# A decoder step on one core: the dense expert stage's loads ordered behind the last projections' loads, and the finishing loads spread over blocks

## The chip, the cores and the metric

The kernel runs on one core of one Trainium2 chip. The core has TensorE (PE in the tables, PEld for its weight loads), VectorE (DVE), ScalarE (ACT), GpSimd (POOL) and SyncE (SP). Here SP computes nothing: it issues nearly all loads and stores, in the order of its program, and an instruction that has to wait holds up everything behind it. GpSimd issues the indirect gathers on a queue of its own. The metric is the device time of one execution in microseconds, as the median of the runs.

## The reference, cut to what matters

One decoder layer is applied to 64 sample tokens and 512 prompt tokens, D = 1024, all in float32. After a mixer (an S5 group and an RWKV-7 group) each token gets a channel mixer that retrieves experts:

```python
x = x + ga1 * (concat([y_s5, y_rw]) @ w_out)
h = rmsnorm(x, norm2_g) * (1 + sc2) + sh2
q = (h @ w_q).reshape(T, 8, 2, 64)                      # 8 heads, two halves of a key
s1, s2 = q[:, :, 0] . keys1, q[:, :, 1] . keys2         # 128 scores each
# top 16 of s1 and of s2, the 256 sums of them, top 16 of these: 16 of 16384 experts per head
act = gelu(u_tab[idx] . h)
ff  = sum over the 8 x 16 chosen experts of gate * act * v_tab[idx]
y   = rmsnorm(x + ga2 * ff, final_norm_g)
```

## The kernel before, in words

The 576 tokens are five tiles: tile 0 holds the 64 sample tokens, tiles 1 to 4 are 128 prompt tokens each. They go through the mixer in the order 1, 2, 3, 0, 4 (`ORDER`), several stages of different tiles woven together by generators.

`select` (L1201) makes a tile's output projection, its norm, the query projection and the scores. It streams its weights through two buffers of 512 KB with the tag "w": eight `wo`, `ga1`, `sh2`, eight `wq` (L1267, used at L1269), and `keys` last (L1273, used at L1285). A load into one of the two buffers waits until PE (or another reader) is done with what was in it. `pick` (L1292) finds the top experts, almost all of it on DVE.

The experts of tiles 1 to 3 (`DENSE`) are not gathered but computed densely. `gbuild` (L1463) writes a table of gates into DRAM (`Gd`), and `dense` (L1538) runs over all 16384 experts in 128 blocks of 128. For block b:
- `ublock` (L1498) loads 512 KB of u (`ur`, two buffers), splits it into a high part on ACT (`uh`, L1504) and a low part on DVE (`ul`, L1505), and PE makes `pd`, 24 matmuls (L1508). `first(b + 1)` calls it one block ahead.
- ACT applies Gelu (`wf`, L1587), DVE multiplies by the gates `Gr` (L1589), and the result is split again (`wh`, `wl`).
- 512 KB of v (`vr`, two buffers, L1599) are loaded and split likewise (`vh`, `vl`), and PE adds 18 matmuls to the sums `po` (L1607).
- `loadG` (L1561) fetches the gates `Gr` of eight blocks at a time, 1536 KB in rows of 512 bytes, into one of two buffers.

Beside the dense blocks go the selection of tile 4 (`pick`, three steps a block) and `bulk` (L1425), which gathers the experts of tiles 0 and 4 row by row: 384 gathers of 512 KB from GpSimd, each consumed by one DVE instruction (L1441 or L1451), three a block. At block 32 (`FB`) `open_finish` (L1389) loads what `finish` (L1404) needs for the last addition and norm of all five tiles: the rows `fx` of each tile, the gates `fg` of prompt and samples, and the norm's weights `gF`.

The program's order on an engine is made when the kernel is built, by a planner that simulates the engines and takes, among what it holds ready, what was traced first. So a load whose buffer is free early may be put ahead of loads that were traced long before it. `tc.issue_after(ins)` adds an order without a wait: what the block traces on the engine of `ins` comes after `ins` in that engine's program.

Of the kernel before, what the change touches and what calls it, by code (L numbers as in the profile page):

```python
# [147 lines left out]
def weave(tc, *parts):  # L148
    live = [[p[0], p[1], 0.0, p[2], p[3] if len(p) > 3 else 0] for p in parts]
    while any(p[3] for p in live):  # L150
        for p in list(live):
            p[2] += p[1]
            while p[2] >= 1:
                p[2] -= 1
                try:
                    if p[4]:
                        with tc.high_priority(offset=p[4]):
                            next(p[0])
                    else:
                        next(p[0])  # L160
                except StopIteration:
                    live.remove(p)
                    break
# [14 lines left out]
class Kernel:  # L178
# [3 lines left out]
    GBL = 8  # L182
# [1018 lines left out]
    def select(self, ti):  # L1201
        yo = self.yo.pop(ti)
        nc, I, O = self.nc, self.I, self.O
        V, S, G, T, SY = nc.vector, nc.scalar, nc.gpsimd, nc.tensor, nc.sync
        t2, t4, ps, ident, sm = self.t2, self.t4, self.ps, self.ident, self.sm
        sw = self.sw
        smp = ti == 0
# [62 lines left out]
                yield  # L1270
            S.copy(qT[:, 4 * q:4 * q + 4, :], pt)
        keys = self.ws.tile([128, 8, 128], F32, name="keys", tag="w", bufs=2)
        SY.dma_start(keys, I["keys"])  # L1273
        sc4 = []
        for g0 in range(0, 4 if smp else 8, 4):
            for sd in range(2):
# [112 lines left out]
    def open_finish(self):  # L1389
        SY = self.nc.sync  # L1390
        self.sf = Scope(self.tc)
        f = self.fin = self.sf.pool("fin", side="right", reuse_waits="tile")
        self.fx = {}
        for ti in list(self.ORDER):
            self.fx[ti] = f.tile([128, D], F32, name="fx%d" % ti)
            SY.dma_start(self.fx[ti], self.x1d[ti])
        self.fg = {}
        for smp in (False, True):
            self.fg[smp] = f.tile([128, D], F32, name="fg%d" % smp)
            self.mod(self.fg[smp], 3, smp)  # L1400
        self.gF = f.tile([128, D], F32, name="gF")
        SY.dma_start(self.gF, self.I["rows"][1:2, :].to_broadcast([128, D]))

    def finish(self, ti, ffs, add=None):  # L1404
        nc, O = self.nc, self.O
        V, S = nc.vector, nc.scalar
        smp = ti == 0
        nr = 64 if smp else 128
        c0 = 0 if smp else 64 + 128 * (ti - 1)
        x1, ga2 = self.fx[ti], self.fg[smp]  # L1410
        tmp = self.fin.tile([128, D], F32, name="ft", bufs=2)
        w = D // len(ffs)
        for n, f in enumerate(ffs):
            V.tensor_tensor(tmp[:nr, n * w:(n + 1) * w], f, ga2[:nr, n * w:(n + 1) * w], op=OP.mult)
        (add or V).tensor_tensor(x1[:nr], x1[:nr], tmp[:nr], op=OP.add)
        ss = self.sm.tile([128, 1], F32, name="ss")
        S.activation(tmp[:nr], x1[:nr], AF.Square, accum_out=ss[:nr])
        self.rstd(ss, ss, 1e-6, nr, self.sm)
        V.scalar_tensor_tensor(x1[:nr], x1[:nr], ss[:nr], self.gF[:nr], op0=OP.mult, op1=OP.mult)
        nc.sync.dma_start(O["y_all"][c0:c0 + nr, :], x1[:nr])  # L1420
# [117 lines left out]
    def dense(self):  # L1538
        nc, I, O = self.nc, self.I, self.O
        V, S, G, T, SY = nc.vector, nc.scalar, nc.gpsimd, nc.tensor, nc.sync  # L1540
        nd, TG, GBL = len(self.DENSE), self.TG, self.GBL
        N = 128 * nd
        S.copy(self.dh, self.hf)
        V.tensor_tensor(self.dl, self.hf, self.dh.bitcast(F32), op=OP.subtract)
        self.sh.close()
        ux = len(self.wu)
        kw = dict(reuse_waits="tile")
        sp = self.sp = Scope(self.tc)
        ue = self.ue if self.EU else sp.pool("ue", **kw)
        up = sp.pool("up", 2, **kw)  # L1550
        dp = self.dp if self.ED else sp.pool("dp", 1, **kw)
        pso = sp.pool("pso", 1, space=PSUM, **kw)
        self.gb = sp.pool("gb", **kw)
        self.tl = sp.pool("tl", **kw)
        outs = []
        for d in range(nd):
            for n in range(2):
                po = pso.tile([128, 512], F32, name="po%d%d" % (d, n))
                outs.append(po)

        def loadG(g):  # L1561
            t = dp.tile([128, N // TG, GBL, TG], F32, name="Gr", bufs=2)
            SY.dma_start(t.rearrange("p g n t -> p g (n t)"),
                         self.Gd[:, :, g * GBL * TG:(g + 1) * GBL * TG].rearrange("g p x -> p g x"))
            return t

        def first(b):
            if b < ux:
                pa = self.wu[b]
                self.mark = None  # L1570
            else:
                if b % 2 and self.PA:
                    pa = self.ps([128, N], "g")
                else:
                    pa = pso.tile([128, 512], F32, name="pd")[:, :N]
                self.ublock(b, pa, up if b % 2 else ue)
            return pa

        pa = first(0)
        G1 = loadG(0)  # L1580
        for b in range(128):
            if b % GBL == 0:
                Gr = G1
            if b % GBL == self.GPF and b + GBL < 128:
                G1 = loadG(b // GBL + 1)
            wf = pa if b < ux else dp.tile([128, N], F32, name="wf", bufs=2)
            S.activation(wf, pa, AF.Gelu)  # L1587
            w3 = wf.rearrange("p (g t) -> p g t", t=TG)
            V.tensor_tensor(w3, w3, Gr[:, :, b % GBL, :], op=OP.mult)  # L1589
            wh = dp.tile([128, N], F32R, name="wh", bufs=2)  # L1590
            wl = dp.tile([128, N], F32R, name="wl", bufs=2)
            S.copy(wh, wf)  # L1592
            mk = V.tensor_tensor(wl, wf, wh.bitcast(F32), op=OP.subtract)  # L1593
            if b < 127:
                pa = first(b + 1)
            if self.mark is None:
                self.mark = mk.ins
            vr = up.tile([128, D], F32, name="vr")
            self.vld = SY.dma_start(vr, I["v_tab"][b * 128:(b + 1) * 128, :])  # L1599
            vh = up.tile([128, D], F32R, name="vh", bufs=1)  # L1600
            vl = up.tile([128, D], F32R, name="vl", bufs=1)
            S.copy(vh, vr)  # L1602
            V.tensor_tensor(vl, vr, vh.bitcast(F32), op=OP.subtract)  # L1603
            for d in range(nd):
                for i, (w, v) in enumerate(((wh, vh), (wh, vl), (wl, vh))):
                    for n in range(2):
                        T.matmul(outs[2 * d + n], w[:, d * 128:(d + 1) * 128], v[:, n * 512:(n + 1) * 512],  # L1607
                                 start=(b == 0 and i == 0), stop=(b == 127 and i == 2))
            yield 0.5 if b < ux else 1.0
        warm = self.sm.tile([128, 1], F32, name="ss")  # L1610
        S.activation(warm, self.iota[:, :1], AF.Sqrt)
        for d in range(nd):
            self.finish(self.DENSE[d], outs[2 * d:2 * d + 2], G if d in self.FP else V)

    def run(self, stop=None):
# [48 lines left out]
        if stop == "mix":  # L1664
            weave(tc, (pk, 1.0, True))
        else:
            dense, gs = self.dense(), self.gathers()
            n = m = 0.0
            for b, r in enumerate(dense):
                m += self.PW  # L1670
                while m >= 1 and pk:
                    m -= 1
                    with tc.issue_after(self.gv.ins):
                        live = next(pk, 0)
                    if live == 0:
                        pk = None
                        self.sx.close()
                if b == self.FB:
                    with tc.issue_after(self.vld.ins):
                        self.open_finish()  # L1680
                n += self.RATE * r * 128 / (128 - 0.5 * len(self.wu))
                with tc.issue_after(self.mark):
                    while n >= 1:
                        next(gs, None)
                        n -= 1
            for _ in gs:
                pass
            self.sp.close()
            self.sf.close()
# [31 lines left out]
```

## Time and profile before

| | us |
|---|---|
| median of 3 runs | 2015.09 |
| lowest and highest of them | 2008.65, 2018.15 |
| the profiled execution | 2014.89 |
| its span in the trace | 2013.1 |

| engine | busy us | share of the span | instructions |
|---|---|---|---|
| PE | 1830.9 | 91% | 11183 |
| PEld | 1585.3 | 79% | 11183 |
| DVE | 1556.4 | 77% | 3052 |
| ACT | 820.3 | 41% | 1496 |
| POOL | 786.9 | 39% | 607 |

The 16 DMA engines moved 514.09 MB at a mean of 255 GB/s. The page cuts the span into 40 slices and gives each engine's busy share in tenths; "PEclk" is the granted clock of PE in tenths of full speed. In a timeline a row is the start, the duration, the engine, the source line, the operation, and in brackets the idle time before it with what ended that.

### The profile page before, as it was taken

The page shows a single profiled execution, that of the slowest core. Times are in us where ns is not written, and L with a number is a line of the kernel's source. Part 1 is how long each engine was busy: PE and PEld are TensorE (multiplying, and loading weights), DVE is VectorE, ACT ScalarE, POOL GpSimd, SP SyncE. Part 2 cuts the span into 40 slices and gives each one's busy share as a digit, 9 for nine tenths or more (in the row PEclk, how much of TensorE's full clock was granted, in tenths as well). Part 3 has the DMA queues.
Part 4 walks back from the last instruction along what each step waited for, and adds up shares of the span by engine and source line. Part 5 has one row for each costly group of instructions (what it writes and reads, how often), then busy time and mean ns, then how long its engine had stood idle before and what let it go on. Part 6 is the DMA issues. An engine that isn't in the chain of part 4 may idle for free.

```text
span 2013.1 us, 30594 instructions
## 1 busy us (share of the span) xinstructions
PE 1830.9 (91%) x11183; PEld 1585.3 (79%) x11183; DVE 1556.4 (77%) x3052; ACT 820.3 (41%) x1496; POOL 786.9 (39%) x607
## 2 busy tenths in 40 slices
PE   7698898999988978649999989899999999999995
PEld 5497755786858767648989979799999999999993
DVE  7959243559699888549988858688888888888887
ACT  4122144354675578613333323433333333333332
POOL 2645211011154234312445534354454445445552
PEclk9799899999989989879999989999999999999998
DMA  7433355233444577657999999699999999999994
GB/s 291 129 111 93 114 197 174 89 134 131 163 157 159 196 246 282 243 196 256 323 347 364 334 324 355 242 358 357 344 326 343 341 350 325 342 337 354 326 319 144
DMA packets 203191, 514.09 MB, mean 255 GB/s; under 512 B 26200, under 2 KB 88792, under 8 KB 198944
## 3 DMA queue, kind: packets, MB, share of 16 engines
q1 hardware_dynamic: 147088, 308.43, 44.1%
q0 software_dynamic: 55584, 202.40, 27.5%
q8 instruction: 88, 1.44, 0.3%
q10 hardware_dynamic: 368, 1.31, 0.2%
q14 instruction: 63, 0.52, 0.1%
HBM read 471.28 MB, written 39.62 MB: 254 GB/s over the span
## 4 chain that ended last, share of the span: by engine, by line
PE 33%; issue 22%; DVE 18%; POOL 15%; DMA 7%; ACT 5%; SPq 1%; POOLq 0%; DVEq 0%; ACTq 0%
POOL gr L1436 14%; PE pd L1508 8%; PE po L1607 8%; PE par L329 3%; PE pas L1269 2%; PE par L1026 2%; PE par L1034 1%; DVE oh L1478 1%; DMA wq<-w_q 1%; PE pas L1229 1%; PE par L1038 1%; PE pag L303 1%; DMA vr<-v_tab 1%; DMA ur<-u_t 1%; DVE ab L1485 1%
## 5 line engine op out<-in xcount | busy, mean ns | idle before, releaser
L1436 POOL DMA_INDIRECT gr<-u_tab,ei x192 | 255.9, 1333 | 309.4 <-DVE scr L1441 204.6
L1436 POOL DMA_INDIRECT gr<-v_tab,ei x192 | 261.0, 1359 | 276.9 <-DVE acc L1451 242.7
L1508 PE MATMUL pd<-dh,uh 128*128 128x384 f32 x1024 | 345.9, 338 | 15.9 <-ACT uh L1504 9.1
L1508 PE MATMUL pd<-dh,ul 128*128 128x384 f32 x1024 | 345.6, 338 | 0.2 <-DVE ul L1505 0.2
L1508 PE MATMUL pd<-dl,uh 128*128 128x384 f32 x1024 | 344.9, 337 | 0.0
L1504 ACT CAST uh<-ur 128x1024 fp32r<-128x1024 f32 x128 | 134.5, 1051 | 299.1 <-PE pd L1508 288.0
L1441 DVE SCALAR_TENSOR_TENSOR scr<-gr,h 128x1024 bf16<-128x1024 f32 x192 | 235.2, 1225 | 15.6 <-DMA gr<-u_tab,ei 13.1
L1451 DVE SCALAR_TENSOR_TENSOR acc<-gr,act,acc 128x1024 f32<-128x1024 f32 x190 | 243.3, 1280 | 2.1 <-DMA gr<-v_tab,ei 0.2
L1607 PE MATMUL po<-vl,wh 128*128 128x512 f32 x768 | 237.9, 391 | 1.2 <-DVE vl L1603 1.2
L1607 PE MATMUL po<-vh,wl 128*128 128x512 f32 x768 | 236.9, 390 | 1.3 <-DVE wl L1593 1.3
L1505 DVE TENSOR_TENSOR ul<-ur,uh 128x1024 fp32r<-128x1024 f32 x128 | 156.7, 1224 | 90.3 <-ACT uh L1504 88.5
L1508 PEld LDWEIGHTS pd<-dh,uh 128*128 128x128 f32 x1024 | 193.7, 189 | 23.9 <-ACT uh L1504 9.4
L1607 PE MATMUL po<-vh,wh 128*128 128x512 f32 x768 | 200.4, 395 | 6.8 <-ACT vh L1602 6.7
L1508 PEld LDWEIGHTS pd<-dl,uh 128*128 128x128 f32 x1024 | 193.6, 189 | 4.9
L1508 PEld LDWEIGHTS pd<-dh,ul 128*128 128x128 f32 x1024 | 193.5, 189 | 1.1 <-DVE ul L1505 0.8
L1592 ACT CAST wh<-wf 128x384 fp32r<-128x384 f32 x128 | 66.0, 515 | 307.4 <-PE po L1607 288.7
L1603 DVE TENSOR_TENSOR vl<-vr,vh 128x1024 fp32r<-128x1024 f32 x128 | 156.3, 1221 | 27.0 <-ACT vh L1602 23.3
L1607 PEld LDWEIGHTS po<-vl,wh 128*128 128x128 f32 x768 | 143.9, 188 | 33.1 <-DVE vl L1603 2.0
L1607 PEld LDWEIGHTS po<-vh,wl 128*128 128x128 f32 x768 | 144.1, 188 | 32.7 <-DVE wl L1593 1.6
L1607 PEld LDWEIGHTS po<-vh,wh 128*128 128x128 f32 x768 | 141.3, 188 | 33.8 <-ACT vh L1602 10.8
L1602 ACT CAST vh<-vr 128x1024 fp32r<-128x1024 f32 x128 | 134.9, 1054 | 51.6 <-PE po L1607 40.9
L1490 POOL TENSOR_TENSOR ab<-oh,dix 128x512 f32<-128x512 bf16 x72 | 88.7, 1235 | 153.6 <-DVE oh L1478 63.1
(473 smaller groups left out, 3277.5 us busy)
## 6 DMA issues: line engine op xcount, KB each, us to landing
ur<-u_t SPq DMA_DIRECT2D x128, 512.0 KB
vr<-v_tab SPq DMA_DIRECT2D x128, 512.0 KB
Gd<-Gst SPq DMA_DIRECT2D x24, 1024.0 KB
Gr<-Gd SPq DMA_DIRECT2D x16, 1536.0 KB
wo<-w_out SPq DMA_DIRECT2D x40, 512.0 KB
wq<-w_q SPq DMA_DIRECT2D x40, 512.0 KB
wt<-w_ada SPq DMA_DIRECT2D x32, 512.0 KB
wr<-w_in SPq DMA_DIRECT2D x18, 512.0 KB
```

The costliest lines, as they stand in the source:

```text
L329: mm = self.nc.tensor.matmul(p, w[:, k, :], h[:, k, c:c + 288], start=(k == 0 and i == 0), stop=(k == KB - 1 and i == 2))
L1436: G.indirect_dma_start(out=r, out_offset=None, in_=I[tab], in_offset=bass.IndirectOffsetOnAxis(ap=ei[:, k:k + 1], axis=0))
L1441: V.scalar_tensor_tensor(scr, r, 1.0, h2, op0=OP.mult, op1=OP.mult, accum_out=act[:, k:k + 1])
L1451: V.scalar_tensor_tensor(acc, r, act[:, k:k + 1], acc, op0=OP.mult, op1=OP.add)
L1490: G.tensor_tensor(A, oh, bc(self.dix[:, 1]), op=OP.mult)
L1504: nc.scalar.copy(uh, ur)
L1505: self.mark = nc.vector.tensor_tensor(ul, ur, uh.bitcast(F32), op=OP.subtract).ins
L1508: nc.tensor.matmul(pa, u[:, k, :], h[:, k, :], start=(k == 0 and i == 0), stop=(k == KB - 1 and i == 2))
L1592: S.copy(wh, wf)
L1602: S.copy(vh, vr)
L1603: V.tensor_tensor(vl, vr, vh.bitcast(F32), op=OP.subtract)
L1607: T.matmul(outs[2 * d + n], w[:, d * 128:(d + 1) * 128], v[:, n * 512:(n + 1) * 512], start=(b == 0 and i == 0), stop=(b == 127 and i == 2))
```

## The change: what it does

`select` keeps its `keys` load as `self.kld`; after the last call this is tile 4's. In `dense`, the loads of `ur`, `Gr` and `vr` are traced inside `issue_after(self.kld.ins)`, so on SP's queue all of them come after that `keys` load. `open_finish` becomes a generator that issues one load (or one pair of halves) per step, from block 32 on one step per block, each behind that block's `vr` load; the order of the finishing loads is now fx of tile 0, fg of the samples, gF, fx of tiles 1, 2, 3, 4, fg of the prompt.

```diff
         keys = self.ws.tile([128, 8, 128], F32, name="keys", tag="w", bufs=2)
-        SY.dma_start(keys, I["keys"])
+        self.kld = SY.dma_start(keys, I["keys"])
...
         for ti in list(self.ORDER):
             self.fx[ti] = f.tile([128, D], F32, name="fx%d" % ti)
-            SY.dma_start(self.fx[ti], self.x1d[ti])
         self.fg = {}
         for smp in (False, True):
             self.fg[smp] = f.tile([128, D], F32, name="fg%d" % smp)
-            self.mod(self.fg[smp], 3, smp)
         self.gF = f.tile([128, D], F32, name="gF")
+        SY.dma_start(self.fx[0], self.x1d[0])
+        yield
+        self.mod(self.fg[True], 3, True)
+        yield
         SY.dma_start(self.gF, self.I["rows"][1:2, :].to_broadcast([128, D]))
+        yield
+        for ti in self.ORDER:
+            if ti:
+                SY.dma_start(self.fx[ti], self.x1d[ti])
+                yield
+        self.mod(self.fg[False], 3, False)
+        yield
...
-        pa = first(0)
-        G1 = loadG(0)
+        with self.tc.issue_after(self.kld.ins):
+            pa = first(0)
+            G1 = loadG(0)
...
-                G1 = loadG(b // GBL + 1)
+                with self.tc.issue_after(self.kld.ins):
+                    G1 = loadG(b // GBL + 1)
...
-                pa = first(b + 1)
+                with self.tc.issue_after(self.kld.ins):
+                    pa = first(b + 1)
...
-            self.vld = SY.dma_start(vr, I["v_tab"][b * 128:(b + 1) * 128, :])
+            with self.tc.issue_after(self.kld.ins):
+                self.vld = SY.dma_start(vr, I["v_tab"][b * 128:(b + 1) * 128, :])
...
-                if b == self.FB:
+                if b >= self.FB:
+                    if b == self.FB:
+                        fl = self.open_finish()
                     with tc.issue_after(self.vld.ins):
-                        self.open_finish()
+                        next(fl, None)
```

## Rows read from the trace of the kernel before

**Rows 1.** The page's 40 slices of the span, two of its rows.

```profile
PE   7698898999988978649999989899999999999995
PEclk9799899999989989879999989999999999999998
```

**Rows 2.** Table by stretch: length, each engine's busy us, PEclk, DMA share, GB/s.

```profile
850.00:890.00 40.00, 14.18 (x92) 13.83 (x93) 5.02 (x10) 1.76 (x4) 9.37 (x9) 0.66 0.83 303
890.00:925.00 35.00, 29.06 (x142) 26.05 (x141) 35.00 (x169) 11.12 (x16) 5.02 (x5) 0.95 0.37 123
925.00:1160.00 235.00, 234.28 (x1186) 213.14 (x1186) 215.08 (x347) 86.36 (x118) 113.24 (x86) 1.00 0.93 333
...
1170.00:1180.00 10.00, 10.00 (x52) 9.04 (x51) 6.38 (x8) 3.44 (x5) 2.62 (x2) 1.00 1.04 417
...
1280.00:1320.00 40.00, 34.69 (x163) 28.30 (x162) 27.34 (x42) 18.41 (x25) 12.52 (x10) 1.00 0.66 225
1320.00:1990.00 670.00, 665.90 (x3348) 602.19 (x3347) 564.15 (x686) 233.72 (x318) 330.45 (x243) 1.00 0.93 334
1990.00:2013.00 23.00, 1.97 (x9) 1.31 (x7) 15.78 (x32) 6.48 (x13) 7.00 (x3) 0.60 0.23 92
```

**Rows 3.** Timeline of SP's queue around the last wq loads: start, us, line.

```profile
840.97 2.21 SPq L1599 DMA_DIRECT2D vr<-v_tab  x2
...
853.28 14.23 SPq L1563 DMA_DIRECT2D Gr<-Gd  x2
867.63 8.13 SPq L1267 DMA_DIRECT2D wq<-w_q  x1
...
883.85 0.33 SPq L1273 DMA_DIRECT2D keys<-keys  x1
905.22 0.33 SPq L1501 DMA_DIRECT2D ur<-u_t  x1
```

**Rows 4.** Timeline of PE, the last projections and the first dense product.

```profile
854.69 5.45 PE L1269 MATMUL pas<-t4s,wq 128*128 128x128 f32 x32 [5.61 <-DMA wq<-w_q]
880.04 6.38 PE L1269 MATMUL pas<-t4s,wq 128*128 128x128 f32 x32 [19.89 <-DMA wq<-w_q]
887.66 2.96 PE L1285 MATMUL pas<-keys,t4s 64*128 64x128 f32 x32 [1.24 <-DMA keys<-keys]
890.57 0.44 PE L1508 MATMUL pd<-dh,uh 128*128 128x384 f32 x1
```

**Rows 5.** Timeline of DVE, the start of the last selection and a split.

```profile
889.44 0.87 DVE L1305 MAX8 vals<-t2s 128x8 f32<-128x128 f32 x4 [22.60 <-ACT t2s L1287]
...
903.98 1.21 DVE L1505 TENSOR_TENSOR ul<-ur,uh 128x1024 fp32r<-128x1024 f32 x1
```

**Rows 6.** Chain of waits in order of time, one block of the dense stage.

```profile
1149.74 4.18 PE pd L1508 x24
1153.92 4.12 PE po L1607 x18
```

**Rows 7.** Timeline of PE behind the finishing loads.

```profile
1196.28 0.69 PE L1508 MATMUL pd<-dh,uh 128*128 128x384 f32 x1 [9.10 <-ACT uh L1504]
...
1203.91 1.55 PE L1607 MATMUL po<-vh,wh 128*128 128x512 f32 x6
```

**Rows 8.** Timeline of SP's queue around the finishing loads.

```profile
1147.93 0.33 SPq L1501 DMA_DIRECT2D ur<-u_t  x1
...
1166.99 3.37 SPq L1396 DMA_DIRECT2D fx<-x1d  x5
...
1176.99 0.34 SPq L1402 DMA_DIRECT2D gF<-rows  x1
1178.77 0.34 SPq L1501 DMA_DIRECT2D ur<-u_t  x1
```

**Rows 9.** Timeline of ACT, two casts of u.

```profile
1162.09 1.05 ACT L1504 CAST uh<-ur 128x1024 fp32r<-128x1024 f32 x1 [2.96 <-PE pd L1508]
...
1195.19 1.05 ACT L1504 CAST uh<-ur 128x1024 fp32r<-128x1024 f32 x1 [7.47 <-DMA ur<-u_t]
```

## The prediction

> **What bounds the kernel now.** I began with the slices of the page [rows 1]. A slice is 50.3 us. TensorE (PE) is at 9 tenths almost everywhere in the second half, which is the dense stage. Just ahead of it stand a 6 and a 4, from 805 to 906 us, with the clock at 8 and 7; the clock has one more 8 inside the dense stage, from 1158 us on. The table by stretch gives sizes [rows 2]. From 1320 to 1990 us PE is busy 665.90 of 670 us at clock 1.00: the dense stage runs at PE's pace, 8.3 us a block (24 matmuls of the first product in 4.18 us, 18 of the second in 4.12 [rows 6]), and what PE loses ahead of it is lost at the end too. From 850 to 890 us PE is busy 14.18 of 40 us at clock 0.66, from 890 to 925 it is 29.06 of 35. The last row, 1990 to 2013, is the finishing tail behind PE, which this change does not touch.
>
> Then I read who waits in the first hole. PE's projections of the last token tile (L1269) wait for their weights wq, 5.61 us and then 19.89 [rows 4]. SyncE's queue shows why [rows 3]. From 841 us on it issues loads of the dense stage, and at 853.28 two Gr loads, whose issue takes 14.23 us; behind them the next wq takes 8.13 us to issue, so it leaves at 875.76 and its product starts at 880.04. The two Gr are early work: DVE waits 22.60 us for the scores of the last tile, then works on their selection from 889.44, and comes to the split of a dense block at 903.98 [rows 5]; the first Gr is wanted only after that.
>
> The second hole: eight finishing loads of 512 KB (five fx, gF, fg of the prompt, fg of the samples in two halves) are issued between 1166.99 and 1177 in one row, and the ur behind them goes out at 1178.77 [rows 8]. ScalarE can cast it at 1195.19 only, after 7.47 us idle [rows 9]; PE waits 9.10 us and then runs 24 matmuls at a lower clock, from 1196.28 to 1203.91 [rows 7].
>
> **The change, part by part.** *Loads behind the last keys.* Every ur, vr and Gr now stands on SyncE's queue behind the keys load of tile 4. Removed are the two blocked issues of 14.23 and 8.13 us ahead of the seventh wq. The wq buffers are two: the seventh goes out when PE has finished the fifth, 854.69 + 5.45/2 = 857.4, and lands 4.3 us later as it did (875.76 to 880.04), so 861.7; the eighth goes out at 860.1, lands at 864.4 and is multiplied by 866.3. The keys load gets its buffer at 863.6 and lands 3.8 us later (883.85 to 887.66), so the keys product starts at 867.4 instead of 887.66: 20 us. Upstream the fifth wq also waited beside vr and ur loads that are now gone, worth 0 to 4 us; before that three early ur loads vanish from beside earlier work, worth 0 to 2 us. I take 22 us, ends 20 and 26.
>
> What this costs: the loads were early, and covered by PE's waiting. Now ur of block 0 is issued just after keys, and its two splits, a 1.05 us cast on ScalarE [rows 9] and a 1.21 us subtraction on DVE [rows 5], stand between it and the product. Before, the first dense product started 2.9 us after the keys product (887.66 to 890.57 [rows 4]); I put it at 6, a loss of 3. Two ul and one vl, 3 x 1.21 = 3.6 us, move from idle DVE time into the stretch where DVE is busy 35.00 of 35 us [rows 2]; most of that overlaps with the 3, and I charge 4 for both. The cover can also fail: behind the added order, Gr is queued among ur and vr on the same engine, and a second Gr's issue can again stop the queue for 14 us, this time ahead of the ur of block 2. So the ends are 0 and 15. GpSimd's gathers are on their own queue and run into the wq loads earlier than before; they did so in this trace as well, so they stand in the 4.3 us.
>
> First part: 22 - 4 = 18 us, ends 20 - 15 = 5 and 26 - 0 = 26.
>
> *Finishing loads, one per block.* Removed: 9.10 us of waiting, and the slow clock behind it, 7.63 us for 24 matmuls against 4.18, so 3.4: in all 12.5. Moved: nine DMAs, 4.19 MB, over nine blocks or 75 us, one behind each vr: 56 GB/s on top of the 333 of the steady stretch, 389 in all. The rows show 417 GB/s between 1170 and 1180 [rows 2], so it fits. A load of 512 KB takes 1.26 us at that rate, and a ur has 14.2 us from issue (1147.93) to its cast (1162.09) [rows 8, 9]; 1.26 us more is covered. If the cover is gone because 333 is all there is, the 4.19 MB take 12.6 us of PE's time and all is given back. I take 12, ends 0 and 12.5.
>
> A rule speaks against this. The Trainium skill, "DMA: Bandwidth & Descriptors", section Specifications, gives about 358 GB/s as a core's share of the HBM. By that figure 389 GB/s does not fit; the 31 missing over 75 us are 2.3 MB, an estimated 6.5 us of stall, the second part would be 6 us instead of 12 and the sum 1991. The trace disagrees with it as a ceiling over 10 us (the 417 GB/s of its row); over 75 us no row here shows more.
>
> *Sum.* The profiled execution took 2014.89 us (its span 2013.1), the median of the runs is 2015.09: 2014.89 - 18 - 12 = 1984.9, so 1985.
>
> **The rivals.** *The ramp gives it back.* The keys come 20 us earlier but the first blocks starve: Gr stops the queue ahead of ur, or selection work on DVE is placed ahead of the first splits, as the 14.5 us between 889.44 and 903.98 [rows 5] were ahead of a ur split. Then the first part is 5 and the sum 2014.9 - 5 - 12 = 1998. For it: the 14.23 us issue, and DVE never idle from 890 to 925. Against it: PE needed that split only as its third block. Chance 0.20.
>
> *The finishing loads find no room.* The transfer engines are shown 0.93 busy over the steady stretch [rows 2]. If the average of 334 GB/s is what can be had with gathers in the mix, the second part is 0 and the time 2014.9 - 18 = 1997. Against it: 417 GB/s for 10 us. The skill's figure above stands for half of this case. Chance 0.09.
>
> *The order changes nothing at the hole.* If wq is late because of the gathers and the Gd writes, and not because of Gr's issue, the wait stays and only the second part counts: 2003. For it: gathers are issued there as well, GpSimd being busy 9.37 of 40 us [rows 2]. Against it: the wq issue itself lasts 8.13 us, just behind Gr. Chance 0.06.
>
> *Slower.* The nine spread loads make nine short stalls instead of one, each with a drop of the clock behind it: 9 x (1.26 + 3.4) = 42 us, less 12.5 and 18 saved, gives 2026. It decides from 3.4 us lost per block. Against it: from 1280 to 1320 PE lost 5.3 us in short waits and the clock stayed 1.00 [rows 2]. Chance 0.03.
>
> **How the numbers follow.** My forecast has 0.60, with its own range from 1977 to 1993; the last 0.02 is for what I have not thought of. The range for the time, 1973 to 2003, takes in the second, third and fourth case and the best ends of both parts (2014.9 - 26 - 12.5 = 1976, less some us since the runs shown spread over 9.5). This kernel's measurement tells about 0.5% from no change, some 10 us. Below 2005 lie the forecast, the second and third case nearly whole and part of the fourth: faster 0.90; same 0.07; slower 0.03.
>
> **What would show it.** Right: no wait of PE for wq longer than about 6 us, no Gr issue ahead of the last wq, the keys product near 866, the first dense product between 869 and 875, and PE without idle time from about 905; near block 32 one fx or fg between neighbouring vr, no wait of PE for uh, and clock 1.00 there; PE's end some 30 us earlier, the tail of 24 us as it is. Wrong for the first part: a wait for uh or Gr, or a long DVE row of selection ahead of the first ul, that lasts past 890. Wrong for the second: PE idle in small pieces through the nine blocks. The prediction as a whole fails if PE waits for ur or vr at many places of the steady stretch, so that the transfers and not PE set its pace.

## The result and the profile after

| | us |
|---|---|
| before, median of 4 runs | 2016.62 |
| after, median of 4 runs (lowest 1980.87, highest 1987.41) | 1982.66 |
| ratio after to before, 95% interval | 0.9836 [0.981, 0.9861] |
| the profiled execution after, its span | 1987.41, 1985.6 |

The time is 34.0 us less, the interval excludes 1, and it lies 2.3 us from the predicted 1985. The profiled execution is the slowest of its four. Its span is 27.5 us shorter than that of before, but the two traces differ already where their programs are still the same. These rows of SyncE's queue (start, duration) are the store of x1 of the last token tile, first before, then after:

```profile
815.68 0.32 SPq L1242 DMA_DIRECT2D x1d<-t4s  x1
```

```profile
820.94 0.32 SPq L1242 DMA_DIRECT2D x1d<-t4s  x1
```

After stands 5.3 us later. Up to a wq load at 735.26 us before and 740.16 us after the two programs have the same order, so 4.9 us are older than the change; from there to the store they take 80.4 and 80.8 us. In the fourteen traces of this document the store lies between 813.7 and 821.1 us, and in before, e2 and e3, whose order is the same up to it, at 815.7, 815.1 and 820.2. So every mark below is counted from this store; by it the end comes 32.7 us earlier (1197.4 to 1164.7).

The page's slices after, which answer to [rows 1]: the 6 and 4 of PE have become 7 and 6 (a slice is 49.6 us now), and the clock's 8 in the dense stage is gone.

```profile
PE   7698898999998988769999999999999999999994
PEclk9799899989999989899999999999999999999997
```

The table by stretch after, as [rows 2]; the stretch from 1147 to 1222 us is that of the finishing loads:

```profile
850.00:890.00 40.00, 25.66 (x165) 23.87 (x163) 16.71 (x78) 8.67 (x13) 6.50 (x7) 0.91 0.95 328
890.00:925.00 35.00, 32.98 (x163) 29.05 (x164) 35.00 (x134) 12.98 (x18) 10.26 (x9) 1.00 0.71 238
925.00:1147.00 222.00, 222.00 (x1126) 202.34 (x1125) 203.19 (x314) 81.54 (x111) 109.29 (x83) 1.00 0.94 337
1147.00:1222.00 75.00, 74.61 (x371) 66.27 (x370) 55.73 (x56) 24.63 (x35) 29.77 (x23) 1.00 1.00 357
1222.00:1320.00 98.00, 97.34 (x485) 86.23 (x484) 77.35 (x96) 40.35 (x56) 37.54 (x30) 1.00 0.87 306
1320.00:1940.00 620.00, 620.00 (x3131) 563.15 (x3131) 525.37 (x646) 217.92 (x297) 307.05 (x231) 1.00 0.95 340
```

PE is busy 25.66 us instead of 14.18 from 850 to 890, at clock 0.91 instead of 0.66, and the dense stage has no hole left. SyncE's queue after, as [rows 3]:

```profile
850.49 9.44 SPq L1267 DMA_DIRECT2D wq<-w_q  x4
866.87 0.33 SPq L1273 DMA_DIRECT2D keys<-keys  x1
867.25 0.43 SPq L1510 DMA_DIRECT2D ur<-u_t  x1
867.77 0.38 SPq L1572 DMA_DIRECT2D Gr<-Gd  x1
868.20 5.98 SPq L1510 DMA_DIRECT2D ur<-u_t  x1
874.23 0.90 SPq L1612 DMA_DIRECT2D vr<-v_tab  x2
875.17 1.02 SPq L1572 DMA_DIRECT2D Gr<-Gd  x1
876.30 7.75 SPq L1510 DMA_DIRECT2D ur<-u_t  x2
```

The last wq loads stand together with nothing of the dense stage among them; the slow issues, 5.98 and 7.75 us, now fall on ur behind each Gr. PE after, as [rows 4] (idle time and its releaser in brackets): the longest wait for wq is 3.58 us instead of 19.89, and the ramp has two short waits.

```profile
863.16 5.47 PE L1269 MATMUL pas<-t4s,wq 128*128 128x128 f32 x32 [3.58 <-DMA wq<-w_q]
870.86 2.23 PE L1285 MATMUL pas<-keys,t4s 64*128 64x128 f32 x24 [2.24 <-DMA keys<-keys]
...
883.34 0.44 PE L1517 MATMUL pd<-dh,uh 128*128 128x384 f32 x1 [4.00 <-ACT wf L1598]
890.92 0.45 PE L1517 MATMUL pd<-dh,uh 128*128 128x384 f32 x1 [1.51 <-ACT uh L1513]
```

The first finishing loads on SyncE's queue after, as [rows 8]: one fx or fg behind a vr, and ur goes out on time.

```profile
1147.74 0.42 SPq L1400 DMA_DIRECT2D fx<-x1d  x1
1149.09 0.33 SPq L1510 DMA_DIRECT2D ur<-u_t  x1
1153.06 0.33 SPq L1612 DMA_DIRECT2D vr<-v_tab  x1
1153.44 0.63 SPq L814 DMA_DIRECT2D fg<-modd  x1
```

**Marks of all runs**, in us after the x1 store: start of the keys product; start of the first dense product; ScalarE's Gelu (wf) of dense block 10, 32, 66 and 127; PE's end; the tail from there to the end of the span; and how many accumulations of gathered rows stand behind the last split (vl) in DVE's order. The last column is the ratio to the kernel before, measured in the same session.

| run | keys | first | 10 | 32 | 66 | 127 | PE end | tail | late | ratio |
|---|---|---|---|---|---|---|---|---|---|---|
| before | 72.0 | 74.9 | 163.6 | 347.4 | 646.6 | 1154.7 | 1176.3 | 21.1 | 0 | 1 |
| after | 49.9 | 53.9 | 143.7 | 326.4 | 609.7 | 1117.5 | 1140.5 | 24.2 | 4 | 0.9836 |
| e1_loads_only | 49.3 | 53.4 | 143.2 | 326.0 | 617.3 | 1124.8 | 1147.1 | 21.1 | 0 | 0.9842 |
| e2_finish_only | 72.8 | 75.7 | 164.4 | 347.2 | 630.5 | 1138.4 | 1160.1 | 21.2 | 0 | 0.9909 |
| e3_gr_only | 60.4 | 65.4 | 156.9 | 339.6 | 623.2 | 1131.1 | 1153.5 | 21.1 | 0 | 0.9873 |
| e4_ur_vr_only | 62.1 | 65.8 | 156.4 | 351.7 | 644.8 | 1152.9 | 1173.5 | 21.1 | 0 | 0.9972 |
| e5_burst_at_36 | 49.7 | 53.9 | 143.6 | 326.4 | 617.0 | 1125.1 | 1146.2 | 21.2 | 1 | 0.9839 |
| e6_gr_later | 49.6 | 53.9 | 146.8 | 340.9 | 627.3 | 1134.0 | 1155.2 | 21.1 | 0 | 0.989 |
| e7_gathers_held | 52.9 | 57.8 | 147.9 | 341.7 | 632.8 | 1140.6 | 1161.7 | 21.2 | 0 | 0.9916 |
| e8_double_dose | 50.4 | 55.1 | 144.9 | 327.6 | 614.7 | 1121.8 | 1144.3 | 26.5 | 6 | 0.9859 |
| e9_gathers_after_wq | 45.2 | 48.9 | 144.0 | 326.4 | 609.0 | 1117.0 | 1139.2 | 24.2 | 4 | 0.9789 |
| e10_vh_two | 50.7 | 54.9 | 146.6 | 338.0 | 623.3 | 1130.0 | 1138.2 | 35.6 | 12 | 0.981 |
| e11_every_second | 49.7 | 53.8 | 146.2 | 329.8 | 613.1 | 1121.0 | 1143.2 | 24.2 | 4 | 0.9792 |
| e12_best | 44.5 | 48.4 | 142.0 | 324.8 | 605.2 | 1112.5 | 1135.8 | 25.5 | 5 | 0.9821 |

How well marks repeat: from block 66 to 127 all fourteen take 506.7 to 508.2 us. Up to block 32, after, e1, e5, e8 and e11 order their work nearly alike, and lie at 326.0 to 329.8. So a difference of 3 us in the ramp is not told apart by one trace, and the ratios, with intervals of some 0.2 to 0.3% to either side, tell less. A mark is set by a block's first product, and where PE's order of products changes, the marks of single blocks move with it; over a whole stretch they are safer.

### The profile page after: what moved, and what is told of

Its sections match the earlier page's. It is cut to its first block, busy times and chain, and to the rows that moved or that the text cites. A ratio compares the mean times of both kernels' runs of the same rounds, so it can differ in the third digit from the quotient of the medians.

```text
span 1985.6 us, 30595 instructions
## 1 busy us (share of the span) xinstructions
PE 1828.2 (92%) x11183; PEld 1581.9 (80%) x11183; DVE 1555.2 (78%) x3052; ACT 817.1 (41%) x1494; POOL 778.2 (39%) x607
## 4 chain that ended last, share of the span: by engine, by line
PE 63%; DVE 18%; issue 6%; DMA 6%; ACT 4%; POOL 3%; SPq 0%; POOLq 0%; DVEq 0%; ACTq 0%
PE pd L1517 23%; PE po L1620 23%; POOL gr L1445 3%; PE par L329 3%; DMA wq<-w_q 2%; PE pas L1269 2%; PE par L1026 1%; PE pas L1229 1%; PE par L1034 1%; DVE oh L1487 1%; PE par L1038 1%; PE pag L303 1%; DVE ab L1494 1%; DMA gr<-v_tab,ei 1%; PE pas L789 1%
## 5 line engine op out<-in xcount | busy, mean ns | idle before, releaser
L1445 POOL DMA_INDIRECT gr<-u_tab,ei x192 | 251.6, 1311 | 303.3 <-DVE scr L1450 229.7
L1513 ACT CAST uh<-ur 128x1024 fp32r<-128x1024 f32 x128 | 134.5, 1051 | 275.4 <-PE pd L1517 257.6
L1514 DVE TENSOR_TENSOR ul<-ur,uh 128x1024 fp32r<-128x1024 f32 x128 | 156.5, 1222 | 101.9 <-ACT uh L1513 101.6
L1620 PEld LDWEIGHTS po<-vl,wh 128*128 128x128 f32 x768 | 143.7, 188 | 33.9 <-DVE vl L1616 2.6
```

What stands on the lines that cost most here:

```text
L1445: G.indirect_dma_start(out=r, out_offset=None, in_=I[tab], in_offset=bass.IndirectOffsetOnAxis(ap=ei[:, k:k + 1], axis=0))
L1513: nc.scalar.copy(uh, ur)
L1514: self.mark = nc.vector.tensor_tensor(ul, ur, uh.bitcast(F32), op=OP.subtract).ins
```

## The experiments

**Which part did it.** e1 keeps the ordered loads and puts the finishing loads back into one row; e2 keeps the spread finishing loads and takes the order away.

```diff
 e1:
-                if b >= self.FB:
-                    if b == self.FB:
-                        fl = self.open_finish()
+                if b == self.FB:
                     with tc.issue_after(self.vld.ins):
-                        next(fl, None)
+                        self.open_finish()
 (and open_finish issues all its loads at once, as before)
 e2, at all four loads:
-            with self.tc.issue_after(self.kld.ins):
-                pa = first(0)
+            pa = first(0)
```

> Only the order behind the keys load; the eight finishing loads go out at block 32 in one row as before. Theory (two independent holes): gains the first part alone, 18 to 22 us, so 1995 to 1998 against 2016.6 before; PE again waits 9 us for uh near block 32 and runs a product at the lower clock. Rival (the steady stretch is set by the transfers, so an early gain is given back later): under 10 us gained, 2007 or more. Rival (what the finishing loads cost depends on where the stretch starts): the wait near block 32 is gone without the spreading, 1983 to 1986.

> Only the finishing loads spread, one per block; ur, vr and Gr go out early as before. Theory (two independent holes): gains 12 to 16 us, 2001 to 2005; PE waits 20 us for wq near 860 as before and not at block 32. Rival (the spread loads find no room beside 333 GB/s): 0 to 6 us gained, 2011 to 2016, with PE waiting in small pieces over nine blocks.

Measured: e1 1989.19 us, ratio 0.9842 [0.9819, 0.9866]; e2 2000.57 us, 0.9909 [0.9886, 0.9933]. PE waits for uh again in e1, 7.80 us (the row stands with e5 below), and 19.9 us for wq in e2, as the theory has it. But e1 is faster than its theory's 1995 to 1998. By the marks the end of e1 is 29.2 us earlier than before's, that of e2 16.1, and of both together 32.7, not 45.3. The marks show why. Blocks 32 to 66 take 299.2 us before, 283.3 after and in e2, and 291.3 in e1: so in e1, too, 7.9 us of what spreading is worth had come without it. One wait of before is missing there, between blocks 44 and 50 (58.7 us before, 52.3 in e1, 53.1 after). PE before, in that stretch:

```profile
1295.47 1.66 PE L1607 MATMUL po<-vh,wh 128*128 128x512 f32 x6 [1.61 <-ACT vh L1602]
1299.73 0.45 PE L1508 MATMUL pd<-dh,uh 128*128 128x384 f32 x1 [2.59 <-ACT wf L1587]
1307.89 1.66 PE L1607 MATMUL po<-vh,wh 128*128 128x512 f32 x6 [0.96 <-ACT vh L1602]
```

PE waits here for ScalarE and not for a transfer; in before's order of PE only 3 and 1 matmuls of a first product stand ahead of two second products at this place. The planner sets the order anew in each kernel, and the place is gone in both. Of the 4.7 us that are left (45.3 - 7.9 = 37.4 against 32.7), 3.6 are lost at the end of the stage (from wf of block 127 to the end: 42.7 us before, 43.4 in e1, 42.9 in e2, 47.2 after), told of below. So on top of the ordered loads the spreading brings 3.5 us by the marks (29.2 to 32.7), and the ratios, 0.9842 and 0.9836, do not tell the two kernels apart.

**Which loads.** e3 orders only Gr behind the keys, e4 only ur and vr; both spread the finishing loads.

```diff
 e3:
+        pa = first(0)
         with self.tc.issue_after(self.kld.ins):
-            pa = first(0)
             G1 = loadG(0)
 (and so for first(b + 1) and vr; the later Gr stay ordered)
 e4:
         with self.tc.issue_after(self.kld.ins):
             pa = first(0)
-            G1 = loadG(0)
+        G1 = loadG(0)
 (and so for the later Gr)
```

> Finishing loads spread; of the dense loads only Gr is ordered behind the keys load, ur and vr are free to go early. Theory (the issue of Gr holds up SyncE's queue, and with it wq): nearly the whole gain stays, 1980 to 1986; the keys product comes no more than 5 us later than with all of them ordered, for the 2 MB of vr and ur beside the wq loads, and the first dense product follows the keys product by 3 us instead of 4. Rival (any bytes of the dense stage moved there delay wq, in proportion): 2 of 5.1 MB stay early, so 40% of 22 us is lost, 1991 or more.

> Finishing loads spread; ur and vr ordered behind the keys load, Gr free to go early. Theory (Gr's issue holds up the queue): two wq stand behind two Gr as before, issues of 14 and 8 us come back, PE waits 15 to 20 us for wq, and only the second part is left: 2000 to 2005. Rival (bytes in proportion): 3.1 of 5.1 MB are early, 60% of 22 us lost, 1996. Rival (it was ur and vr that held wq): 1983 to 1987.

Measured: e3 1995.6 us, ratio 0.9873 [0.985, 0.9897]; e4 2012.45 us, 0.9972 [0.9952, 0.9993]. SyncE's queue and then PE in e4:

```profile
844.92 14.54 SPq L1572 DMA_DIRECT2D Gr<-Gd  x2
859.56 4.88 SPq L1267 DMA_DIRECT2D wq<-w_q  x2
```

```profile
868.29 5.32 PE L1269 MATMUL pas<-t4s,wq 128*128 128x128 f32 x32 [14.00 <-DMA wq<-w_q]
875.79 2.96 PE L1285 MATMUL pas<-keys,t4s 64*128 64x128 f32 x32 [2.18 <-DMA keys<-keys]
```

PE in e3, where no Gr stands ahead of wq:

```profile
860.49 6.78 PE L1269 MATMUL pas<-t4s,wq 128*128 128x128 f32 x32 [5.47 <-DMA wq<-w_q]
871.55 6.38 PE L1269 MATMUL pas<-t4s,wq 128*128 128x128 f32 x32 [4.29 <-DMA wq<-w_q]
880.54 5.10 PE L1285 MATMUL pas<-keys,t4s 64*128 64x128 f32 x32 [2.60 <-DMA keys<-keys]
```

The Gr loads go and the keys product comes 11.6 us earlier; ur and vr go and it comes 9.9 us earlier; both, 22.1. The two Gr are 2 x 1536 KB, 3.1 MB, or 3.7 us per MB; the four ur and vr loads among wq from 841 us on [rows 3] are 2.1 MB, or 4.7 us per MB. With 3 us of scatter in a trace these two prices are not told apart; at the 303 GB/s moved from 850 to 890 us [rows 2] one MB takes an estimated 3.3 us. So bytes ahead on the queue delay wq, whichever load they belong to: the rival of e3, and not my theory that Gr's issue alone stops the queue. With Gr away, every wq up to the keys is issued in under 0.5 us, and PE still waits 5.47 and 4.29 us behind ur and vr.

The long issue is a mark of Gr all the same. From 800 us on, 219 issues on SyncE's queue in the fourteen traces took over 2 us; 215 of them are the issue directly behind a Gr load, and the other four stand one place further on. Of the 14.23 us in [rows 3] the first Gr took 0.38 and the second, behind it, 13.81; in e4 the two took 0.38 and 14.11. That such a stop costs wq more than the bytes do is not shown: the price per MB is no higher for Gr than for ur and vr.

In e4 the gain is lost again: wf of block 32 comes 4.3 us later than before's. PE waits 19 times for vh from 860 us on, 16.3 us in all, in an order with at most 6 matmuls of a first product ahead of the second products of blocks 3 to 17.

**The row of finishing loads elsewhere.** e5 issues it at block 36, away from Gr's load.

```diff
 e1, and:
-    FB = 32
+    FB = 36
```

> The changed kernel with its nine finishing loads issued in one row again, but at block 36 instead of 32, four blocks away from the load of the next Gr. Theory A (the burst hurts because it falls together with the 1 MB Gr load; in block 32 of the kernel before the two stood 20 us apart): with the Gr away the burst is covered, PE waits for a ur under 3 us, the ratio to the kernel before is that of the changed kernel, 0.984, or up to 0.002 less since the nine blocks at 8.70 us go away. Theory B (4.19 MB in one row stop the queue by themselves, some 9 to 12 us at the rate shown there): PE waits 7 to 9 us for a ur in the block behind block 36, followed by a stretch at a lower clock, and the ratio is 0.984 to 0.988.

Measured: 1987.57 us, ratio 0.9839 [0.9818, 0.986]. PE waits for a ur here as in e1. PE in e1, then in e5:

```profile
1178.96 0.69 PE L1508 MATMUL pd<-dh,uh 128*128 128x384 f32 x1 [7.80 <-ACT uh L1504]
```

```profile
1207.20 0.69 PE L1508 MATMUL pd<-dh,uh 128*128 128x384 f32 x1 [5.40 <-ACT uh L1504]
```

The wait, 5.40 us, lies between theory A's 3 and theory B's 7 to 9, and the granted clock falls to 0.5 behind it, as B has it. Blocks 32 to 66 take 290.6 us, 7.3 more than after and 0.7 less than e1. That speaks for theory B: the row costs nearly its price away from Gr's load too (1536 KB, not the 1 MB of the expectation). The ratio alone decides nothing, since it fits both theories: 3.0 us come back in the tail and 1.6 ahead of PE's end, and the rest is within the interval.

**How much room.** e8 issues each finishing load twice.

```diff
-                SY.dma_start(self.fx[ti], self.x1d[ti])
+                for _ in range(2):
+                    SY.dma_start(self.fx[ti], self.x1d[ti])
 (and so for the other finishing loads)
```

> The changed kernel with each of the nine finishing loads issued twice into the same tile: 8.4 MB over nine blocks instead of 4.2. It asks how much room the steady stretch has. If the transfer engines can give some 417 GB/s there, as over 10 us of the kernel before: 333 + 112 = 445 are asked, 28 short over 75 us, 2.1 MB or 5 us lost, ratio 0.986. If 358 GB/s is all (a figure of the Trainium skill, DMA: Bandwidth & Descriptors, section Specifications): 87 short over 75 us, 6.5 MB or 18 us lost, ratio 0.992; by that figure the single dose would already have lost 6. If the loads that run ahead (ur and vr are issued 10 to 14 us before they are wanted) absorb it: no loss, 0.984.

Measured: 1989.71 us, ratio 0.9859 [0.9839, 0.9878]; blocks 32 to 66 take 3.8 us more than after. The first answer gave 5 us and 0.986. Its reason, a shortage spread over 75 us, is not shown: PE's waits of over 1 us there are 1.09 and 2.68 us at 1219.6 and 1222.9 us, in the product of a ur whose issue, directly behind a Gr load, took 11.33 us. The table by stretch of e8:

```profile
1142.00:1222.00 80.00, 76.43 (x383) 68.36 (x381) 55.53 (x58) 26.16 (x36) 29.17 (x22) 1.00 1.03 371
```

It moves 371 GB/s over 80 us, with PE losing 3.6 us: more than the 357 of after. The single dose therefore did not fill what there is.

**The gathers' bytes.** e7 was to hold GpSimd's load of h and the gathers behind it until the last wq product.

```diff
 e7 (self.qTl is the last projection's output):
+        if smp:
+            G.tensor_tensor(h2[:, 0:1], self.qTl[:, 7, 0:1], self.qTl[:, 7, 0:1], op=OP.mult)
 e9, ahead of each of the first five gathers:
+            if smp and tab == "u_tab" and k < 5:
+                G.tensor_tensor(r[:, 0:1], self.qTl[:, 7, 0:1], self.qTl[:, 7, 0:1], op=OP.mult)
```

> The changed kernel with one added GpSimd instruction ahead of the first gathers of tile 0, which reads the last projection's output: the load of h and five gathers, some 3.1 MB, so go out after the last wq product and not beside its loads. Theory (what delays wq is every byte ahead of it on the shared transfer engines, whichever queue it came by, 3.7 to 4.7 us per MB as the two halves of the order showed): the keys product comes 5 to 12 us earlier, against the last load of tile 4's stage, and the time is that much less, 1974 to 1981 for a kernel before of 2019. Rival (only what stands ahead in SyncE's own queue delays it): the keys product stays within 2 us of the changed kernel's, and the time as well, unless the gathers, now beside the first ur and vr loads, lengthen the ramp by up to 10 us.

It held h alone: the planner put five gathers ahead of it, from 832.79 us on. The keys product came 3.0 us later, and blocks 10 to 18 took 77.5 us instead of 67.0, in another order; 2000.34 us, ratio 0.9916 [0.9896, 0.9937]. So it was no test of the theory, and e9 held the gathers themselves:

> The changed kernel with one added GpSimd instruction ahead of each of the first five gathers of the samples' tile; it reads the last projection's output, so that the five gathers (2.6 MB) go out when the last wq is done. (The run in which only the load of h was held let those gathers out 10 us earlier instead, and the keys product came 3 us later.) Theory (every byte ahead on the shared transfer engines delays wq, at 3.7 to 4.7 us per MB): the keys product comes 5 to 12 us earlier against the last store of the stage ahead, 38 to 45 us after it instead of 49.9, and the time falls by as much, less what the gathers now cost the ramp. Rival (only SyncE's own queue counts): 48 to 51 us and the changed kernel's time, ratio 0.984.

Measured: 1982.9 us, ratio 0.9789 [0.9758, 0.982]. The keys product came 45.2 us after the store, 4.7 earlier than after, just short of the expected 5; in e12, which has the same edit, 44.5 us, while the seven kernels that order all the loads and leave the gathers alone lie at 49.3 to 50.7. So bytes of another queue count too, at 4.7 us for 2.6 MB, 1.8 us per MB; PE's waits for wq that are left are 0.53 to 1.87 us each, so its own pace caps what more could be gained, and the 1.8 is a lower bound. But at block 10 nothing is left of it (144.0 against 143.7). SyncE's queue and PE in e9:

```profile
865.97 14.23 SPq L1513 DMA_DIRECT2D ur<-u_t  x2
```

```profile
878.31 0.69 PE L1520 MATMUL pd<-dh,uh 128*128 128x384 f32 x1 [6.27 <-ACT wf L1601]
```

The gathers now meet the ramp's loads, and two ur take 14.23 us to issue, 13.75 of them the one directly behind the second Gr: the first of the rivals, on a small scale. The ratio is lower than the changed kernel's because the kernel before took 2027.52 us in that session, which e10 and e11 share; the two kernels' own times, 1982.9 and 1982.66, don't differ, and by the marks e9 ends 1.3 us earlier.

**The ramp.** e6 loads the second Gr two blocks later.

```diff
-    GPF, PA, DO = 2, False, 20000
+    GPF, PA, DO = 4, False, 20000
-                with self.tc.issue_after(self.kld.ins):
+                with self.tc.issue_after(self.vld.ins):
                     G1 = loadG(b // GBL + 1)
```

> The changed kernel with the load of the next group's Gr issued at block 4 of each group, behind that block's vr, instead of block 2 and behind the keys alone; so the second Gr no longer stands ahead of the ur loads of the ramp. Theory (the ramp loses its few us because Gr's issue holds ur up 6 to 8 us there): PE's waits for wf and uh in the first three dense blocks (4.0 and 1.5 us in the changed kernel) shrink, the ramp gains 2 to 4 us, ratio 0.982. Rival (the ramp is held by ScalarE and DVE, which do the splits one after another): the waits stay and the time is within 2 us of the changed kernel's. If Gr comes too late at block 4, PE waits for it or for the wf made from it once in each group, up to 15 x 2 us more.

Measured: 1995.79 us, ratio 0.989 [0.9873, 0.9907]; by the marks the end is 11.6 us later than after's. The ramp did gain: wf of block 4 came 89.4 us after the store instead of 95.2. Then an order with at most 4 matmuls of a first product ahead of the second products of blocks 3 to 14 took it back and more; block 18 came at 224.6 instead of 210.7, and PE waited 15 times for vh, 15.0 us in all.

**The order of PE's products.** In after, the six blocks 34 to 39 have such an order. PE, then ScalarE, after:

```profile
1178.15 0.62 PE L1620 MATMUL po<-vh,wl 128*128 128x512 f32 x2
1178.60 0.33 PE L1517 MATMUL pd<-dh,uh 128*128 128x384 f32 x1
...
1179.48 0.34 PE L1517 MATMUL pd<-dh,ul 128*128 128x384 f32 x1
1179.90 0.50 PE L1620 MATMUL po<-vh,wh 128*128 128x512 f32 x1
```

```profile
1178.35 0.52 ACT L1603 CAST wh<-wf 128x384 fp32r<-128x384 f32 x1 [4.92 <-PE po L1620]
1178.80 1.05 ACT L1615 CAST vh<-vr 128x1024 fp32r<-128x1024 f32 x1
...
1187.05 0.52 ACT L1603 CAST wh<-wf 128x384 fp32r<-128x384 f32 x1 [5.76 <-PE po L1620]
```

There is one vh buffer. It comes free when the last second product is done, and the next wants the new vh six matmuls later, after 1.1 us, instead of 24 matmuls and 4.2 us later. The 1.05 us cast does not fit, and a block takes 8.70 us (1178.35 to 1187.05) instead of the steady 8.31. e10 gives vh two buffers; e11 puts a finishing load into every second block.

```diff
 e10:
-            vh = up.tile([128, D], F32R, name="vh", bufs=1)
+            vh = up.tile([128, D], F32R, name="vh", bufs=2)
 e11:
-                if b >= self.FB:
+                if b >= self.FB and (b - self.FB) % 2 == 0:
```

> The changed kernel with two buffers for vh instead of one. Theory (in blocks 35 to 40 the written order lets PE run only 6 matmuls of the first product between two second products, 1.1 us, which is less than the 1.05 us cast into the one vh buffer with its waits; so each block takes 8.70 us instead of 8.31): the waits of PE for vh go, 2 to 3 us are gained, ratio 0.982 to 0.983. Rival (the order is set anew with the buffer, and its luck decides): the waits move to other blocks and the time stays within 3 us of the changed kernel's.

> The changed kernel with the finishing loads in every second block: 4.2 MB over 17 blocks or 140 us, 30 GB/s on top instead of 56. Theory (the loads themselves are covered at one a block; what is left of the second part is the order of the products): the time stays within 2 us but for blocks 35 to 40, where the written order has two such short blocks instead of six, 1.5 us less; ratio 0.983. Rival (the transfers have too little room at one a block): PE's period comes back to 8.31 us in all 17 blocks and 3 us or more are gained, ratio 0.982.

Measured: e10 1989.34 us, ratio 0.981 [0.9779, 0.9841]; e11 1986.13 us, 0.9792 [0.9766, 0.9818]. In e10 no wait for vh is left among PE's waits and PE ends 2.3 us earlier than after, as the theory has it; but the tail grows by 11.4 us, with twelve accumulations behind the last split. Its Gelus run nearer to PE's end (8.2 us from block 127 instead of 23.0), so its other marks can't be compared. e11 takes 283.3 us from block 32 to 66 like after: neither the 1.5 us of the theory nor the 3 of the rival (three short blocks are left, 34 to 36, where the theory had two). Room was not what one load a block lacked. e12 is e9 with the finishing loads from block 34 on, where the order came out without a row of short blocks:

```diff
 e9, and:
-    FB = 32
+    FB = 34
```

> The run with the five gathers held behind the last wq, and its nine finishing loads spread from block 34 on instead of 32. In the written order of PE no row of short blocks (6 instead of 24 matmuls of the first product ahead of a second product) stands in the dense stage any more, but five accumulations of gathered rows, instead of the changed kernel's four, stand behind the last split on DVE. Theory (the order of the products, not the loads, takes the 3 us of the second part, and each late accumulation costs the tail some 1 us): PE's end 2 to 3 us earlier against the last store of the stage ahead than in the changed kernel (1137.5 to 1138.5 instead of 1140.5), the tail 25 us instead of 24.2, the end 1162 to 1164, the ratio 0.980 to 0.983. Rival (the loads do not fit at one a block): short waits of PE for vh or uh in blocks 34 to 43 take 3 us as before.

Measured: 1981.79 us, ratio 0.9821 [0.9804, 0.9839]. Blocks 32 to 66 take 280.4 us instead of 283.3, with the same loads, and PE has no wait in them that the profile shows. PE ends 4.7 us earlier than after, 1.6 of which are there at block 32 already; the tail is 25.5 us. By the trace the end comes 3.4 us earlier; by the runs it can't be told from after.

## Why the prediction was right, step by step

**Loads behind the keys: 18 us predicted, 21.0 at block 32.** The term for the keys product was 22 and measured 22.1. Its working is wrong in one step. I put 20 us on "the two blocked issues of 14.23 and 8.13 us" and 0 to 4 on the vr and ur loads among wq. e3 and e4 measure 11.6 and 9.9. I priced the stop of the queue behind Gr at nearly the whole hole; ur and vr, whose own issues did not stop it, have nearly as much of the hole as Gr. The sum held because the whole hole closed, whichever load had made it, and that is luck as far as the two terms go. Of the 0 to 2 us for the three early ur loads nothing shows (80.4 and 80.8 us up to the store).

The charge for the ramp, 4 us, was somewhat large. From the keys product to block 10 after takes 93.8 us and before 91.6; to block 32, 276.5 and 275.4. So 2.2 were lost and half came back. What shows there is what was named: ur held up behind Gr (5.98 and 7.75 us), and waits of 4.00 and 1.51 us for wf and uh.

**Finishing loads: 12 us predicted, 15.9 from block 32 to 66.** The wait for uh, 9.10 us, and the slow matmuls behind it, 3.4 us, are gone, and the clock is 1.00 from 1147 to 1222 us. Besides, three waits of before between blocks 44 and 50, 5.2 us, went with the old order; [rows 2] showed that loss from 1280 to 1320 us and I did not count it, since the diff does not name it. In all PE's waits from block 32 to 66 fall from 14.5 us to 0.6, and with the 3.4 that makes 17.3; the six short blocks, at 8.70 instead of 8.31 us, take some 2 of it back.

On the transfers, my sum asked for 389 GB/s, and 357 were moved, with PE busy 74.61 of 75 us. Of the 32 that are missing 30 are the gathers'. GpSimd's queue (packets, MB, share of the engines' time), before from 925 to 1160 us, then after from 1147 to 1222:

```profile
q0 software_dynamic: 11935, 43.45, 50.8%
```

```profile
q0 software_dynamic: 3186, 11.61, 41.5%
```

That is 185 GB/s before and 155 after, while GpSimd waited 43.7 of the 75 us for DVE to be done with gathered rows. So this trace does not test whether 389 fit; what it shows is that the nine loads cost PE no wait.

The figure that I weighed against it is about 358 GB/s (the Trainium skill, "DMA: Bandwidth & Descriptors", section Specifications). It is no ceiling here: e8 shows 371 GB/s over 80 us. The same page of the Trainium skill says in its section Bandwidth that a core gets about that figure when both cores of a memory domain stream, and that a core alone measured up to 425 GB/s. This kernel runs on one core, so that sentence was the one to weigh; the 417 GB/s over 10 us [rows 2] agree with it, and no run here has a second core.

**The tail: unchanged predicted, 3.1 us longer.** (By the mark of PE's end it was 21.1 us before, not the 24 that I wrote.) DVE at the end of before and then after:

```profile
1987.58 1.23 DVE L1603 TENSOR_TENSOR vl<-vr,vh 128x1024 fp32r<-128x1024 f32 x1 [4.28 <-ACT vh L1602]
2000.53 1.22 DVE L1414 TENSOR_TENSOR ft<-acc,fg 128x1024 f32<-128x1024 f32 x1
```

```profile
1957.03 1.23 DVE L1616 TENSOR_TENSOR vl<-vr,vh 128x1024 fp32r<-128x1024 f32 x1 [0.35 <-ACT vh L1615]
1958.17 1.28 DVE L1460 SCALAR_TENSOR_TENSOR acc<-gr,act,acc 128x1024 f32<-128x1024 f32 x1
1960.63 1.28 DVE L1460 SCALAR_TENSOR_TENSOR acc<-gr,act,acc 128x1024 f32<-128x1024 f32 x1
1963.02 2.18 DVE L1460 SCALAR_TENSOR_TENSOR acc<-gr,act,acc 128x1024 f32<-128x1024 f32 x1
1966.00 2.48 DVE L1460 SCALAR_TENSOR_TENSOR acc<-gr,act,acc 128x1024 f32<-128x1024 f32 x1
```

Before, DVE has done the gathered rows ahead of PE's last block; after, four accumulations stand behind the last split, among the finishing work. Over the fourteen kernels the tail follows their number: 21.1 or 21.2 us for 0 or 1, 24.2 for 4, 25.5 for 5, 26.5 for 6, 35.6 for 12. I read the tail as work behind PE that nothing changes. But all seven kernels whose PE ends at 1146.2 us or earlier have late accumulations, and the seven at 1147.1 or later have none. So I take the tail to be also where the background work surfaces once the dense stage has become shorter than it; no run here changed that alone.

**The sum.** From the store on 32.7 us were gained against 30 predicted: 21.0 to block 32, 15.9 to block 66, 0.3 to block 127, less 4.5 from there to the end (42.7 to 47.2); PE ends 35.8 us earlier where I had some 30. Both mechanisms of the change are there, but that the sum lies so near is in part luck: the 5.2 us of waits that I had not counted and the 4.5 lost at the end, which I had put at nothing, nearly cancel. By the runs the gain is 34.0 us, counted from 2016.62 and not from the 2014.89 of my sum.

**The rivals.** That the ramp gives it back is refuted for the change, and shown as a mechanism by e9, whose 4.7 us are gone at block 10. That the loads find no room, that the order changes nothing, and the nine stalls with clock drops: none of them shows. What remains open is why the planner puts short blocks where it does; moving a DMA by two blocks (e6) or a buffer (e10) moved them, and I have no rule for where.

## What to carry to other kernels

When a load is late, count the megabytes that were issued ahead of it, on every queue, and ask of each whether it is wanted later; the long issue in the queue's timeline is the place to look, not the price, and here it came from the load ahead of it. Read waits as soon as an order is changed: another order of PE's products cost from 3 us (after against e12) to 14 us (e6, at block 32) here, more than most terms of a careful sum. And where one stage gets shorter, look for what ran beside it and now ends last.

## What the runs showed of the hardware

- Bytes ahead on SyncE's own queue delayed a load by 3.7 to 4.7 us per MB (e3, e4, one trace each), those of GpSimd's gathers by at least 1.8 us per MB (e9).
- Behind a Gr load, 1536 KB in rows of 512 bytes, the next issue on SyncE's queue mostly took 2 to 14 us (215 of 224 cases) instead of 0.33, whichever load it was: wq (8.13), Gr (14.11 in e4) or ur (13.75 in e9). Behind no other load from 800 us on did it take over 2 us, save four issues one place further on.
- One core moved 371 GB/s over 80 us with PE busy 76.43 of them (e8).
- The same order of work up to the x1 store took 815.1, 815.7 and 820.2 us (e2, before, e3): a spread of 5 us, a quarter of what the first part gained.
